# Two mixer layers on one core: the four input projections, three split products or one plain fp32 product

## The chip, the cores and the metric

The kernel runs on one core of a Trainium2 chip. The metric is the device time of one execution in microseconds (us). The core's engines are TensorE (PE in the rows; PEld is its weight load), VectorE (DVE), ScalarE (ACT), GpSimd (POOL) and SyncE (SP, which here only issues DMAs). Each engine runs its own list of instructions in the written order and waits on the others by semaphores.

## The reference, cut to what matters

Two layers over x, 512 tokens of 1024 features, all in fp32. Each layer is a mixer and a feed-forward part:

```python
def hybrid_mixer(x, w_in, ...):
    h = x @ w_in                      # 1024 -> 1824 columns
    (s5_u, g_q, g_k, g_v, g_r, g_lf, g_lb, a_q, a_k, a_v) = jnp.split(h, points, axis=-1)
    y_a = s5_mixer(s5_u, ...)         # state space scan, 256 channels
    y_b = gla_mixer(g_q, g_k, g_v, g_r, g_lf, g_lb, ...)   # gated linear attention, 256
    y_c = swa_mixer(a_q, a_k, a_v, swa_sink)               # windowed attention, 512
    return jnp.concatenate([y_a, y_b, y_c], axis=-1) @ w_out

for l in range(2):
    x = layer_norm(ALPHA * x + hybrid_mixer(x, ...), ...)
    hid = jnp.square(jax.nn.relu(x @ w_ff1[l]))
    x = layer_norm(ALPHA * x + hid @ w_ff2[l], ...)
```

The change touches the product `x @ w_in` alone: how it is computed, and what is kept of x for it.

## The kernel before, in words

**Products.** Nearly all large products are made of three: both operands are split into a high part in a rounded fp32 format (fp32r) and the rest, and `mm3` (lines 251 to 254) adds low x high, high x low and high x high in PSUM. Some small products (the GLU at lines 847 and 851, the gates at line 610, attention times values at line 968) are plain fp32: one `matmul` call on unsplit operands.

**Weights.** `wunit` (lines 237 to 249) brings 1024 columns of weights: a DMA by SyncE into one of two `raw` buffers, a copy by ScalarE into the high half of one of six places in `WA` (line 247, recorded at line 221, the helper `copyA`), and a subtraction by VectorE or GpSimd into the low half (line 248). Which of the two does it is written in the table `CFG`: "g0" to "g3" are the four projections, one letter a unit. The places are used in turn, `state["pair"]` modulo 6.

**The input.** `transpose_x` (lines 256 to 276) transposes a tile of 128 tokens on TensorE, eight blocks of 128, copies each half by ScalarE into `M.XT` (line 265) and subtracts on VectorE (line 266). `M.XT` is two tiles of 16 KB a partition under two of the three rotating tags P, Q, R. The same function serves the feed-forward part, with `sums`.

**The projections.** `proj` (lines 347 to 360) makes one group of columns for all 512 tokens: four weight units, then for each of four token tiles eight blocks of 128 features, each an `mm3`. There are four groups a layer: wg1 (the S5 input and the values of the linear attention, 512 columns), wg0 (its queries, keys and gate inputs, 288), wg2 (keys, values and gate of the two attentions, 512), wg3 (the queries of windowed attention, 512). Their results are taken from PSUM by `evac_g0` to `evac_g2` and `mk_evac_g3`.

**The order.** `CFG["seq"]` (line 39) writes the order of the steps of each mixer: in layer 0 "u st0 g0 tb st1 gates scan scores states sink g2 out g3 y keys late s5o w0 ...". "tb" builds the S5 tables (`tb_params`, `tables`), long chains of small VectorE operations, with a share on GpSimd; those of layer 1 are built during the feed-forward part of layer 0. "st0" and "st1" turn the input into states by the tables, "scan" runs over the states (lines 759 to 764 and on), "gates" and "scores" belong to the linear attention, "keys" and "w0" to "w3" to windowed attention (its first products are at line 933). A planner then orders the instructions of each engine by its own estimate of when each is ready, with the written order as the priority, so the steps overlap.

**Places used by others.** The queries of windowed attention lie in two of the six places, its keys in one, and the weights of `w_out` and of the feed-forward part in all, through the same `wunit`.

Of the kernel before, what the change touches and what calls it, by code (L numbers as in the profile page):

```python
# [20 lines left out]
DEPTH = 2  # L21
# [33 lines left out]
    "sa": "VVVV",  # L55
    "g0": "GGGG",
    "g1": "VVVG",
    "g2": "GVVV",
    "g3": "VVVV",
}  # L60
# [4 lines left out]
def trunk(tc, I, out, dbg=None):  # L65
# [73 lines left out]

    M = NS()  # L140

    def new_lt():
# [94 lines left out]
    def wunit(src, eng=None, cuts=1):  # L237
        n = src.shape[-1]
        raw = rawp.tile([128, 1024], F32, tag="raw", name="raw")
        i = state["pair"] % 6  # L240
        state["pair"] += 1
        for j in range(cuts):
            c = slice(n * j // cuts, n * (j + 1) // cuts)
            nc.sync.dma_start(raw[:, c], src[:, c])
        for j in range(cuts):
            c = slice(n * j // cuts, n * (j + 1) // cuts)
            copyA(WA[:, i, 0, c], raw[:, c])
            (eng or V).tensor_tensor(WA[:, i, 1, c], raw[:, c], WAf[:, i, 0, c], op=SUB)  # L248
        return WA[:, i, 0, :n], WA[:, i, 1, :n]

# [4 lines left out]

    def transpose_x(tt, sums=False):
        for h in range(2):
            ps = psB("xt")
            for k in range(4):
                kk = 4 * h + k  # L260
                T.transpose(ps[:, k * 128:(k + 1) * 128], XR[:, tt, kk * 128:(kk + 1) * 128], ident)
            sl = slice(tt * 128, tt * 128 + 128)
            p4 = ps.rearrange("p (k t) -> p k t", k=4)
            t = M.XT[h]
            state["xt%d" % tt] = S.activation(out=t[:, :, 0, sl], in_=p4, func=AF.Copy)
            V.tensor_tensor(t[:, :, 1, sl], p4, t.bitcast(F32)[:, :, 0, sl], op=SUB)
            if not sums:
                continue
            hs = slice(tt % 2 * 128, tt % 2 * 128 + 128)
# [4 lines left out]
        if sums and tt >= 2:  # L274
            for h in range(2):
                tt_(E("xs", h), Tr[2 + h][:, :, hs], Tr[1][:, :, hs], XF[:, h, :, hs], SUB)
# [69 lines left out]

    def proj(src, n, evac, eng, pre=[]):
        units = pre + [wunit(src[kp], E(eng, kp)) for kp in range(len(pre), 4)]
        for tp in range(2):
            ps = psA("proj")  # L350
            for a in range(2):
                tt = 2 * tp + a
                sl = slice(tt * 128, tt * 128 + 128)
                for k in range(8):
                    w = units[k // 2]
# [534 lines left out]
    def swa_keys(p):  # L890
        kps = psA("kT")
        for tt in range(4):
            for v in range(2):
                T.transpose(kps[:, v, tt * 128:tt * 128 + 128], kdt(tt)[:, v].rearrange("p u d -> p (u d)"), ident)
        KH, KL = [WA[:, p, i].rearrange("p (v t) -> p v t", v=2) for i in range(2)]
        copyA(KH, kps)
        V.tensor_tensor(KL, kps, KH.bitcast(F32), op=SUB)
        return KH, KL
# [137 lines left out]
    def ff1_pair(l, i):  # L1036
# [13 lines left out]
        def unit(src, half=None):  # L1050
            if half != 1:
                u = state["pair"] % 6
# [6 lines left out]
            copyA(WA[:, u, 0, c], src)  # L1059
            V.tensor_tensor(WA[:, u, 1, c], src, WAf[:, u, 0, c], op=SUB)  # L1060
            return WA[:, u, 0, c], WA[:, u, 1, c]

# [92 lines left out]
    pre.append(wunit(I["wg1"][0][1], E("g0", 1), CFG["cut"][1]))  # L1155
    for tt in range(1, 4):
        nc.sync.dma_start(XR[:, tt], I["x"][tt * 128:tt * 128 + 128, :])
    transpose_x(0)
    tb_params()
    run(tb0, 1)  # L1160
    for tt in range(1, 4):
        transpose_x(tt)

# [12 lines left out]
    for l in range(DEPTH):  # L1176
        base = state["pair"] - (2 if l == 0 else 0)
        state["l"] = l
        if l:
            scratch_early()  # L1180
        run(proj(I["wg1"][l], 512, evac_g1, "g0", [] if l else pre))
# [18 lines left out]
        steps = {"u": lambda: s5_u(l), "st0": lambda: s5_states(l, 0), "tb": tb_rest, "st1": lambda: s5_states(l, 1),  # L1200
                 "g0": lambda: run(proj(I["wg0"][l], 288, evac_g0, "g1")), "gates": lambda: gla_gates(l),
                 "scan": lambda: s5_scan(l), "scores": lambda: gla_scores(l), "states": lambda: gla_states(l),
                 "sink": sink, "g2": lambda: run(proj(I["wg2"][l], 512, evac_g2, "g2")), "out": lambda: gla_out(l),
                 "g3": lambda: run(proj(I["wg3"][l], 512, mk_evac_g3(Qs), "g3")), "y": lambda: gla_y(l),
                 "keys": keys, "late": scratch_late, "s5o": lambda: s5_out(l)}
# [15 lines left out]
        def after1(tt):  # L1221
            layer_norm(tt, CFG["ln"][tt])
            transpose_x(tt, True)
        out_half1(ylhs, units, ks, ALPHA, after1)
        new_sums()
        for i in range(3):
            split_sum(i)

        def after2(tt, l=l):
            if l + 1 < DEPTH:  # L1230
                layer_norm(tt, CFG["ln2"][tt])
                transpose_x(tt)
# [110 lines left out]
```

## Time and profile before

| | |
|---|---|
| median of 3 runs | 1246.17 us (1239.97 to 1248.57) |
| profiled execution | 1247.4 us, its span 1245.6 us |
| mean granted TensorE clock | 0.977 of full |
| TensorE busy | 1169.3 us, 94% |
| VectorE busy | 901.5 us, 72% |
| ScalarE busy | 553.4 us, 44% |
| GpSimd busy | 164.1 us, 13% |

Stages in the span: layer 0's mixer runs from 0 to about 240 us, its feed-forward part to about 650, layer 1's mixer to about 870, then the second feed-forward part. A busy TensorE is not TensorE at its peak: matmuls overlap, so the pace of a product is read from the starts of consecutive ones, not from the duration of one.

### The profile page before, as it was taken

The page shows a single profiled execution, that of the slowest core. Times are in us where ns is not written, and L with a number is a line of the kernel's source. Part 1 is how long each engine was busy: PE and PEld are TensorE (multiplying, and loading weights), DVE is VectorE, ACT ScalarE, POOL GpSimd, SP SyncE. Part 2 cuts the span into 40 slices and gives each one's busy share as a digit, 9 for nine tenths or more (in the row PEclk, how much of TensorE's full clock was granted, in tenths as well). Part 3 has the DMA queues.
Part 4 walks back from the last instruction along what each step waited for, and adds up shares of the span by engine and source line. Part 5 has one row for each costly group of instructions (what it writes and reads, how often), then busy time and mean ns, then how long its engine had stood idle before and what let it go on. Part 6 is the DMA issues. An engine that isn't in the chain of part 4 may idle for free.

```text
span 1245.6 us, 18803 instructions
## 1 busy us (share of the span) xinstructions
PE 1169.3 (94%) x7400; PEld 985.5 (79%) x7400; DVE 901.5 (72%) x1727; ACT 553.4 (44%) x937; POOL 164.1 (13%) x123
## 2 busy tenths in 40 slices
PE   6696978999999999999999989799999999999997
PEld 4684765678888889989987867556898898998986
DVE  8986988659875675758564399883987485764957
ACT  4253247534522543725533535572465272461640
POOL 3422352112000000000141020220400000000000
PEclk9898999999999999999999999899999999999999
DMA  6340431113453532412422414302144142250331
GB/s 219 103 153 9 73 123 52 52 34 105 123 166 143 159 104 68 150 54 69 153 82 74 158 34 66 122 17 85 35 138 150 51 142 79 88 164 20 100 121 68
DMA packets 50616, 121.68 MB, mean 98 GB/s; under 512 B 13280, under 2 KB 20320, under 8 KB 50528
## 3 DMA queue, kind: packets, MB, share of 16 engines
q1 hardware_dynamic: 37680, 103.53, 25.2%
q10 hardware_dynamic: 12848, 16.95, 5.3%
q8 instruction: 58, 0.95, 0.3%
q14 instruction: 30, 0.25, 0.1%
HBM read 110.53 MB, written 8.88 MB: 96 GB/s over the span
## 4 chain that ended last, share of the span: by engine, by line
PE 67%; DVE 9%; DMA 2%; ACT 2%; issue 1%; SPq 1%; ACTq 0%; DVEq 0%
PE o L252 11%; PE o L253 11%; PE o L254 11%; PE f1s L252 6%; PE f1s L254 6%; PE f1s L253 6%; PE so L968 2%; PE proj L253 1%; PE proj L254 1%; PE proj L252 1%; PE f1e L253 1%; PE pT L962 1%; PE f1e L254 1%; PE f1e L252 1%; DVE XR L319 1%
## 5 line engine op out<-in xcount | busy, mean ns | idle before, releaser
L221 ACT ACTIVATE WA<-raw 128x1024 fp32r<-128x1024 f32 (+2 forms) x129 | 132.4, 1029 | 140.7 <-DMA raw<-in_w_ff 39.2
L248 DVE TENSOR_TENSOR WA<-raw,WA 128x1024 fp32r<-128x1024 f32 (+1 forms) x102 | 121.8, 1195 | 89.8 <-ACT WA L221 89.8
L221 ACT ACTIVATE WA<-MA 128x1024 fp32r<-128x1024 f32 (+1 forms) x72 | 64.5, 913 | 138.4 <-PE o L254 102.2
L979 DVE SCALAR_TENSOR_TENSOR XR<-XR,o 128x512 f32<-128x512 f32 (+1 forms) x81 | 52.7, 676 | 90.4 <-PE o L254 90.3
L1060 DVE TENSOR_TENSOR WA<-MA,WA 128x1024 fp32r<-128x1024 f32 (+1 forms) x72 | 74.4, 1043 | 17.0 <-ACT WA L221 17.0
L252 PE MATMUL f1s<-xs,WA 128*128 128x256 f32 x288 | 81.6, 283 | 0.2 <-DVE MA L230 0.2
L254 PE MATMUL f1s<-xs,WA 128*128 128x256 f32 x288 | 81.5, 283 | 0.0
L253 PE MATMUL f1s<-xs,WA 128*128 128x256 f32 x288 | 81.5, 283 | 0.0
L248 POOL TENSOR_TENSOR WA<-raw,WA 128x1024 fp32r<-128x1024 f32 (+2 forms) x27 | 61.4, 2280 | 130.0 <-ACT WA L221 123.6
L230 POOL TENSOR_TENSOR XR<-XR,lt 128x512 f32<-128x512 f32 (+1 forms) x13 | 18.5, 1421 | 394.1 <-ACT XR L218 394.1
L230 DVE TENSOR_TENSOR MA<-MA,f1s 128x256 f32<-128x256 f32 x120 | 49.6, 418 | 28.6 <-PE f1s L254 19.6
L252 PE MATMUL o<-WA,yYa 128*128 128x512 f32 (+1 forms) x162 | 64.0, 395 | 0.8 <-DVE XR L979 0.7
L253 PE MATMUL o<-WA,yQ 128*128 128x512 f32 (+1 forms) x164 | 63.4, 386 | 0.0
L252 PE MATMUL o<-WA,yQ 128*128 128x512 f32 (+1 forms) x164 | 63.3, 386 | 0.0
L252 PE MATMUL o<-WA,yYb 128*128 128x512 f32 (+1 forms) x162 | 63.0, 389 | 0.0
L253 PE MATMUL o<-WA,yYa 128*128 128x512 f32 (+1 forms) x162 | 63.0, 389 | 0.0
L253 PE MATMUL o<-WA,yYb 128*128 128x512 f32 (+1 forms) x162 | 63.0, 389 | 0.0
L254 PE MATMUL o<-WA,yYb 128*128 128x512 f32 (+1 forms) x162 | 62.8, 389 | 0.0
L252 PE MATMUL o<-WA,yP 128*128 128x512 f32 x160 | 62.8, 392 | 0.0
L254 PE MATMUL o<-WA,yYa 128*128 128x512 f32 (+1 forms) x162 | 62.7, 387 | 0.0
L254 PE MATMUL o<-WA,yQ 128*128 128x512 f32 (+1 forms) x164 | 62.7, 385 | 0.0
L253 PE MATMUL o<-WA,yP 128*128 128x512 f32 x160 | 62.7, 392 | 0.0
(460 smaller groups left out, 3566.0 us busy)
## 6 DMA issues: line engine op xcount, KB each, us to landing
raw<-in_w_ff SPq DMA_DIRECT2D x80, 512.0 KB, 3.5
MA<-in_w_ff SPq DMA_DIRECT2D x48, 512.0 KB, 3.5
raw<-in_wg SPq DMA_DIRECT2D x23, 512.0 KB, 4.0
raw<-in_w_out SPq DMA_DIRECT2D x16, 512.0 KB, 3.9
scr_out<-MA SPq DMA_DIRECT2D x8, 512.0 KB, 3.7
yc<-scr_out ACTq DMA_DIRECT2D x8, 512.0 KB, 4.4
raw<-in_wg SPq DMA_DIRECT2D x8, 288.0 KB, 2.9
MA<-in_s5cb ACTq DMA_DIRECT2D x8, 256.0 KB, 4.2
```

Of the source, the lines that this page charges most:

```text
L221: S.activation(out=o_, in_=i_, func=AF.Copy)
L230: eng.tensor_tensor(o_, a, b, op=op)
L248: (eng or V).tensor_tensor(WA[:, i, 1, c], raw[:, c], WAf[:, i, 0, c], op=SUB)
L252: T.matmul(ps, a[1], b[0], start=first, stop=False)
L253: T.matmul(ps, a[0], b[1], start=False, stop=False)
L254: T.matmul(ps, a[0], b[0], start=False, stop=last)
L319: V.scalar_tensor_tensor(x[:, c], x[:, c], mean, M.lng[:, c], op0=SUB, op1=MUL)
L962: T.transpose(ps[:, b * 128:b * 128 + 128], P[:, h, b * 128:b * 128 + 128], ident)
L968: T.matmul(ps[64 * v:64 * v + 64, :], av[:, tt - 1 + b0 + b, 64 * v:64 * v + 64], M.pT[v][:, b].rearrange("p h q -> p (h q)"), start=(b == ...
L979: V.scalar_tensor_tensor(x, x, scale, ps, op0=MUL, op1=ADD)
L1060: V.tensor_tensor(WA[:, u, 1, c], src, WAf[:, u, 0, c], op=SUB)
```

## The change

The four projections of both mixers are made of one plain fp32 product for each block, on unsplit operands. The weights of a projection unit go by DMA straight into half a place (`runit`), so a place holds two units, and nothing copies or splits them. The transposed input of a mixer is kept once, in fp32 (`M.XF32`, one 16 KB tile under one tag), by ScalarE's copy alone. The six places become six tiles with tags W0 to W5, so that a place can hold either format; the query places, the key place and the first place of `w_out` are renumbered. The feed-forward part and `w_out` stay in three products.

```diff
-    WA = sb.tile([128, 6, 2, 1024], F32R, name="WA")
-    WAf = WA.bitcast(F32)
...
+    def place(i, dt=F32R):
+
+        return sb.tile([128, 2, 1024], dt, tag="W%d" % (i % 6), name="w%d" % (i % 6))
+
...
+    def runit(src, cuts=1):
+
+        n = src.shape[-1]
+        a = state["half"] % 2
+        if a == 0:
+            state["run"] = place(state["half"] // 2, F32)
+        w = state["run"]
+        state["half"] += 1
+        for j in range(cuts):
+            c = slice(n * j // cuts, n * (j + 1) // cuts)
+            nc.sync.dma_start(w[:, a, c], src[:, c])
+        return w[:, a, :n]
...
+            if not split:
+                state["xt%d" % tt] = S.activation(out=M.XF32[:, 4 * h:4 * h + 4, sl], in_=p4, func=AF.Copy)
+                continue
...
-    def proj(src, n, evac, eng, pre=[]):
-        units = pre + [wunit(src[kp], E(eng, kp)) for kp in range(len(pre), 4)]
+    def proj(src, n, evac, pre=[]):
+        units = pre + [runit(src[kp]) for kp in range(len(pre), 4)]
...
-                    mm3(ps[:, a, :n], xt(k, sl),
-                        (w[0][:, c:c + n], w[1][:, c:c + n]), k == 0, k == 7)
+                    T.matmul(ps[:, a, :n], M.XF32[:, k, tt * 128:tt * 128 + 128], units[k // 2][:, c:c + n],
+                             start=(k == 0), stop=(k == 7))
...
-    new_xt(rot[0:2])
+    M.XF32 = big(rot[0], [128, 8, 512], F32, "xf")
+    state["half"] = 0
...
-    pre.append(wunit(I["wg1"][0][0], E("g0", 0), CFG["cut"][0]))
+    pre.append(runit(I["wg1"][0][0], CFG["cut"][0]))
...
-        base = state["pair"] - (2 if l == 0 else 0)
+        base = state["pair"]
+        if l:
+            state["half"] = 2 * base
...
-        qp = [WA[:, (base + 4 + i) % 6] for i in range(2)]
+        qp = []
 
         def Qs(tt):
+            if tt // 2 == len(qp):
+                qp.append(place(base + 2 + tt // 2))
             return qp[tt // 2][:, tt % 2]
...
-            M.KHL = swa_keys(base % 6)
+            M.KHL = swa_keys((base + 4) % 6)
...
-        state["pair"] = base + 14
+        state["pair"] = base + 5
...
-                transpose_x(tt)
+                transpose_x(tt, False)
...
+                if l + 1 < DEPTH:
+                    M.XF32 = big(rot[1], [128, 8, 512], F32, "xf")
```

The entries "g0" to "g3" of `CFG` go with the splits.

## Rows read from the trace of the kernel before

**Rows 1.** The page's 40 equal slices of the span: busy tenths.

```profile
PE   6696978999999999999999989799999999999997
...
DVE  8986988659875675758564399883987485764957
```

**Rows 2.** Busy us by stage: PE, PEld, DVE, ACT, POOL; clock, DMA share, GB/s.

```profile
0.00:60.00 60.00, 39.57 (x187) 32.41 (x187) 53.58 (x171) 18.74 (x33) 25.84 (x23) 0.95 0.52 167
60.00:114.00 54.00, 48.85 (x502) 42.38 (x502) 40.38 (x69) 25.81 (x51) 14.79 (x11) 0.89 0.27 89
114.00:187.00 73.00, 59.35 (x398) 43.60 (x398) 65.65 (x162) 25.74 (x43) 30.40 (x29) 0.91 0.36 87
...
661.00:715.00 54.00, 53.05 (x391) 45.91 (x391) 15.13 (x26) 24.23 (x44) 4.57 (x3) 0.97 0.39 126
715.00:785.00 70.00, 62.02 (x501) 47.34 (x501) 68.38 (x171) 29.28 (x47) 12.53 (x8) 0.98 0.33 79
```

**Rows 3.** The same for TensorE's instructions on the projections' PSUM tile alone.

```profile
0.00:60.00 60.00, 33.89 (x150) 0.95 0.52 167
60.00:114.00 54.00, 20.68 (x90) 0.89 0.27 89
114.00:187.00 73.00, 37.60 (x144) 0.91 0.36 87
...
661.00:715.00 54.00, 43.72 (x215) 0.97 0.39 126
715.00:785.00 70.00, 37.72 (x145) 0.98 0.33 79
```

**Rows 4.** Prices: from the chain, line 847 alone, the timeline of TensorE, the chain.

```profile
811.21 1.77 PE glg L847 x4
...
L847 PE MATMUL glg<-xl,TAB x16: 592/592/648, 206.9 to 821.3; 128*128 128x512 f32 x16
...
84.81 1.99 PE L610 MATMUL gz<-yb 128*128 128x256 f32 x8
86.46 0.58 PE L253 MATMUL proj<-WA,XTQ 128*128 128x512 f32 x1
...
684.39 0.14 PE proj L252
684.53 0.13 PE proj L253
...
751.25 0.23 PE proj L252
751.48 0.23 PE proj L253
```

**Rows 5.** Subtractions of lines 248 and 266, first 130 us: durations min/median/max, starts, forms.

```profile
L248 DVE TENSOR_TENSOR WA<-raw,WA x8: 750/1216/1225, 31.2 to 84.1; 128x1024 fp32r<-128x1024 f32 x5, 128x576 fp32r<-128x576 f32 x3
...
L248 POOL TENSOR_TENSOR WA<-raw,WA x7: 1263/2361/2433, 5.7 to 51.5; 128x1024 fp32r<-128x1024 f32 x4, 128x512 fp32r<-128x512 f32 x2, 128x576 fp32r<-128x576 f32 x1
...
L266 DVE TENSOR_TENSOR XTP<-xt,XTP x4: 682/684/693, 7.7 to 20.5; 128x512 fp32r<-128x512 f32 x4
```

**Rows 6.** Small VectorE operations in the timeline, two held and one not.

```profile
5.72 1.25 DVE L396 SCALAR_TENSOR_TENSOR yc<-yc 128x32 f32<-128x32 f32 x1
...
51.61 2.37 DVE L485 TENSOR_SCALAR A8S<-APW 128x32 f32<-128x32 f32 x1
...
40.49 0.18 DVE L484 COPY AIS<-APW 128x32 f32<-128x32 f32 x1
```

**Rows 7.** Timelines and line 933: the scan's start, SyncE's loads, ScalarE's wait, the scores.

```profile
114.00 0.61 DVE L761 TENSOR_TENSOR yb<-yc,APW 128x256 f32<-128x256 f32 x1
...
624.10 84.63 SPq L244 DMA_DIRECT2D raw<-in_wg  x16
...
706.05 1.06 ACT L221 ACTIVATE WA<-raw 128x1024 fp32r<-128x1024 f32 x1 [3.25 <-DMA raw<-in_wg]
...
L933 PE MATMUL sc<-WA x32: 362/418/582, 188.1 to 233.7; 128*128 128x256 f32 x16, 128*128 128x384 f32 x16
```

More of the change, by code (lines that the diff above doesn't have):

```diff
@@ L55 @@
     "sa": "VVVV",
[L56 to L59, printed above, removed]
 }
@@ L239, in wunit @@
         raw = rawp.tile([128, 1024], F32, tag="raw", name="raw")
-        i = state["pair"] % 6
+        w = place(state["pair"])
+        wf = w.bitcast(F32)
         state["pair"] += 1
@@ L246, in wunit @@
             c = slice(n * j // cuts, n * (j + 1) // cuts)
-            copyA(WA[:, i, 0, c], raw[:, c])
-            (eng or V).tensor_tensor(WA[:, i, 1, c], raw[:, c], WAf[:, i, 0, c], op=SUB)
-        return WA[:, i, 0, :n], WA[:, i, 1, :n]
+            copyA(w[:, 0, c], raw[:, c])
+            (eng or V).tensor_tensor(w[:, 1, c], raw[:, c], wf[:, 0, c], op=SUB)
+        return w[:, 0, :n], w[:, 1, :n]
+    def runit(src, cuts=1):
[9 more added lines that the diff above has]
+        return w[:, a, :n]
     def mm3(ps, a, b, first, last):
@@ L254, in mm3, with transpose_x @@
         T.matmul(ps, a[0], b[0], start=False, stop=last)
-    def transpose_x(tt, sums=False):
+    def transpose_x(tt, split=True):
+        sl = slice(tt * 128, tt * 128 + 128)
+        hs = slice(tt % 2 * 128, tt % 2 * 128 + 128)
         for h in range(2):
@@ L261, in transpose_x @@
                 T.transpose(ps[:, k * 128:(k + 1) * 128], XR[:, tt, kk * 128:(kk + 1) * 128], ident)
-            sl = slice(tt * 128, tt * 128 + 128)
             p4 = ps.rearrange("p (k t) -> p k t", k=4)
+            if not split:
+                state["xt%d" % tt] = S.activation(out=M.XF32[:, 4 * h:4 * h + 4, sl], in_=p4, func=AF.Copy)
+                continue
             t = M.XT[h]
-            state["xt%d" % tt] = S.activation(out=t[:, :, 0, sl], in_=p4, func=AF.Copy)
+            copyA(t[:, :, 0, sl], p4)
             V.tensor_tensor(t[:, :, 1, sl], p4, t.bitcast(F32)[:, :, 0, sl], op=SUB)
-            if not sums:
-                continue
-            hs = slice(tt % 2 * 128, tt % 2 * 128 + 128)
             if tt < 2:
@@ L273, in transpose_x @@
                 tt_(V, Tr[h][:, :, hs], p4, (XF[:, 0] if h == 0 else Tr[0])[:, :, hs], SUB)
-        if sums and tt >= 2:
+        if split and tt >= 2:
             for h in range(2):
@@ L352, in proj @@
                 tt = 2 * tp + a
-                sl = slice(tt * 128, tt * 128 + 128)
                 for k in range(8):
-                    w = units[k // 2]
                     c = (k % 2) * n
-                    mm3(ps[:, a, :n], xt(k, sl),
-                        (w[0][:, c:c + n], w[1][:, c:c + n]), k == 0, k == 7)
+                    T.matmul(ps[:, a, :n], M.XF32[:, k, tt * 128:tt * 128 + 128], units[k // 2][:, c:c + n],
+                             start=(k == 0), stop=(k == 7))
                 evac(tt, ps[:, a, :n])
@@ L894, in swa_keys @@
                 T.transpose(kps[:, v, tt * 128:tt * 128 + 128], kdt(tt)[:, v].rearrange("p u d -> p (u d)"), ident)
-        KH, KL = [WA[:, p, i].rearrange("p (v t) -> p v t", v=2) for i in range(2)]
+        w = place(p)
+        KH, KL = [w[:, i].rearrange("p (v t) -> p v t", v=2) for i in range(2)]
         copyA(KH, kps)
@@ L1051, in unit @@
             if half != 1:
-                u = state["pair"] % 6
+                u = place(state["pair"])
                 state["pair"] += 1
@@ L1058, in unit @@
             c = slice(0, 1024) if half is None else slice(512 * half, 512 * half + 512)
-            copyA(WA[:, u, 0, c], src)
-            V.tensor_tensor(WA[:, u, 1, c], src, WAf[:, u, 0, c], op=SUB)
-            return WA[:, u, 0, c], WA[:, u, 1, c]
+            copyA(u[:, 0, c], src)
+            V.tensor_tensor(u[:, 1, c], src, u.bitcast(F32)[:, 0, c], op=SUB)
+            return u[:, 0, c], u[:, 1, c]
         wa, w12, w3 = unit(r1), unit(s12), unit(r2)
@@ L1152, in trunk @@
     nc.sync.dma_start(XR[:, 0, 0:512], I["x"][0:128, 0:512])
-    pre.append(wunit(I["wg1"][0][0], E("g0", 0), CFG["cut"][0]))
+    pre.append(runit(I["wg1"][0][0], CFG["cut"][0]))
     nc.sync.dma_start(XR[:, 0, 512:], I["x"][0:128, 512:])
-    pre.append(wunit(I["wg1"][0][1], E("g0", 1), CFG["cut"][1]))
+    pre.append(runit(I["wg1"][0][1], CFG["cut"][1]))
     for tt in range(1, 4):
         nc.sync.dma_start(XR[:, tt], I["x"][tt * 128:tt * 128 + 128, :])
-    transpose_x(0)
+    transpose_x(0, False)
     tb_params()
@@ L1180, in trunk @@
             scratch_early()
-        run(proj(I["wg1"][l], 512, evac_g1, "g0", [] if l else pre))
+        run(proj(I["wg1"][l], 512, evac_g1, [] if l else pre))
         if l == 0:
             run(tb0, 2)
-        qp = [WA[:, (base + 4 + i) % 6] for i in range(2)]
+        qp = []
         def Qs(tt):
+            if tt // 2 == len(qp):
+                qp.append(place(base + 2 + tt // 2))
             return qp[tt // 2][:, tt % 2]
@@ L1200, in trunk @@
         steps = {"u": lambda: s5_u(l), "st0": lambda: s5_states(l, 0), "tb": tb_rest, "st1": lambda: s5_states(l, 1),
-                 "g0": lambda: run(proj(I["wg0"][l], 288, evac_g0, "g1")), "gates": lambda: gla_gates(l),
+                 "g0": lambda: run(proj(I["wg0"][l], 288, evac_g0)), "gates": lambda: gla_gates(l),
                  "scan": lambda: s5_scan(l), "scores": lambda: gla_scores(l), "states": lambda: gla_states(l),
-                 "sink": sink, "g2": lambda: run(proj(I["wg2"][l], 512, evac_g2, "g2")), "out": lambda: gla_out(l),
-                 "g3": lambda: run(proj(I["wg3"][l], 512, mk_evac_g3(Qs), "g3")), "y": lambda: gla_y(l),
+                 "sink": sink, "g2": lambda: run(proj(I["wg2"][l], 512, evac_g2)), "out": lambda: gla_out(l),
+                 "g3": lambda: run(proj(I["wg3"][l], 512, mk_evac_g3(Qs))), "y": lambda: gla_y(l),
                  "keys": keys, "late": scratch_late, "s5o": lambda: s5_out(l)}
@@ L1222, in after1 @@
             layer_norm(tt, CFG["ln"][tt])
-            transpose_x(tt, True)
+            transpose_x(tt)
         out_half1(ylhs, units, ks, ALPHA, after1)
@@ L1231, in after2 @@
                 layer_norm(tt, CFG["ln2"][tt])
-                transpose_x(tt)
+                transpose_x(tt, False)
             else:
```

## The prediction

> **What bounds the kernel now.** I read the page's 40 slices first. They show that outside the two mixers TensorE is at nine tenths or more, while in the mixers (the first seven slices and slices 21 to 27) TensorE falls to six and seven tenths and VectorE rises to nine [rows 1]. The table by stage says which engine holds which part [rows 2]. In layer 0 VectorE is busy 53.6 of the first 60 us: it builds the S5 tables there, a chain of small operations. The scan of the S5 states, which needs those tables, begins at 114.0 us [rows 7]. From 114 to 187 both engines are near full: VectorE 65.7 and TensorE 59.4 of 73 us. At 188.1 the first attention scores start [rows 7]. In layer 1 there are no tables to build in the mixer: TensorE alone is full from 661 to 715 (53.1 of 54 us, VectorE 15.1), and from 715 to 785 VectorE leads (68.4 of 70) with TensorE at 62.0 [rows 2]. So the change trades time on one near-full engine for time on the other, and the answer differs by stage.
>
> The same table for the projections alone [rows 3] counts what stands where. A layer has 4 projections x 4 token tiles x 8 blocks = 128 products of three instructions, 384. In layer 0, 240 of these (80 products: all of the first two projections and 16 of the third) come before 114 us, 144 (48 products) after it. In layer 1, 145 (48) come after 715 and 239 (80) before.
>
> **The price of a product.** Three split instructions of 512 columns start 0.23 us apart [rows 4]: 0.69 us a product. With 288 columns they are 0.133 apart on average [rows 4]: 0.40. A plain fp32 product stands in the trace in the GLU: four rows of line 847 take 1.77 us, 0.4425 each [rows 4]. But the source has 2 layers x 2 halves x 2 blocks = 8 such products and the trace has 16 rows [rows 4]: one plain product is two instructions. So it costs 0.885 us, not 0.4425. For 288 columns no row exists. Eight rows of 256 columns (four products) take 1.65 us up to the next projection product, 0.206 each [rows 4]; by columns that is 0.23 for 288, and from the 512 row 0.25. I take 0.24, so 0.48 a product, bounds 0.46 and 0.50. TensorE therefore gains no time, it loses it: per layer 96 x (0.885 - 0.69) + 32 x (0.48 - 0.40) = 18.7 + 2.6 = 21.3 us, and 42.6 us in all.
>
> The Trainium skill (Perfetto Trace Analysis, section Engine Utilization) gives the array's output rate with a factor of one half for its two-part fp32 mode. Read per product, that would be near 0.44 us and the whole change would free TensorE; read per instruction it agrees with the 0.4425 us row, and the count of 16 rows decides for the second reading. The first is kept as the fourth case below.
>
> **What is removed.** Per layer: 16 copies on ScalarE (about 1.05 us, 0.69 for the narrow ones; off the path nearly everywhere), the subtractions behind them, and 8 subtractions of the transposed input on VectorE (0.68 us each; four of the eight are shown) [rows 5]. In layer 0 before the scan VectorE loses 8 weight subtractions, five of 1.22 and three of 0.75 us [rows 5], and those 8: with the small overlap that back-to-back rows show, about 12.5 us. GpSimd loses seven [rows 5], and these cost VectorE too: while one runs, a VectorE operation of 0.18 us takes 1.25 or 2.37 us [rows 6]: the first two rows there are the first and the last of those that were held, the third a free one. Over the seven subtractions I count such excess as 1.1, 1.0, 2.1, 2.2, 1.9, 1.1 and 2.2, about 11 us; the least it could be worth is nothing, if another GpSimd operation takes the place. VectorE's part of the table chain is so 12.5 to 24 us shorter, and I take 24: every held operation is a link of that chain.
>
> **Layer 0.** By VectorE alone the scan starts at 114 - 24 = 90 us. TensorE must keep up: of its 88.4 us before 114 [rows 2] 54.6 are projections [rows 3], so 33.8 are other work. New: 32 x 0.885 + 32 x 0.48 + 33.8 = 77.5 us, against some 84 that lie between the first loads (about 6 us, an estimate) and 90. That fits, with room for 7 products of the third projection instead of 16. The second stage then has 48 + 9 = 57 products, 50.4 us, beside 59.4 - 37.6 = 21.8 us of other work: 72.2 us of TensorE. VectorE needs about 63 there (65.7 less two subtractions). How long the stage lasts hangs on how well TensorE is packed. At the share of before (59.4 of 73, 81%) it is 89 us; at the 98% that TensorE reaches from 661 to 715 it is 74. I take 90%, 80 us. The scores would begin at about 170 instead of 187: **-17 us**, bounds -8 and -23.
>
> **Layer 1.** The start gains a little: the first products no longer wait for a subtraction after each copy, nor for the weights' split, and the GpSimd subtractions leave the layer norm ahead of them. On the other side the first two projections take 32 x 0.195 + 32 x 0.08 = 8.8 us more of a full TensorE. Up to 715 the projections had 49.7 us there, 6.0 before 661 (the remaining 24 instructions, by the same pace) and 43.7 after [rows 3]; the 64 products now need 43.7, so about 7 to 9 of the third projection fit instead of 16. The gates get 3 us back: ScalarE's copy of a weight at 706.05 sat 3.25 us waiting for its load, with the gates queued behind it on that engine [rows 7]. I put the start of the scan 3 us earlier. After it come 55 products, 48.7 us, plus 62.0 - 37.7 = 24.3: 73.0 us of TensorE. At before's 88.6% that is 82.4 us, at 98% 74.5, at 93% 78.5 against 70 now. Together **+5.5 us**, bounds +1.5 and +9.4.
>
> **What moves and what waits.** The 16 weight loads of a layer go straight into the six places, two to a place, where before each went through a ring of two buffers, and SyncE sat 84.6 us over the 16 loads of layer 1 [rows 7]. A load now waits for the last product that read its place. By the count of places (layer 1 begins at place 92, so 2, 3, 4, 5, 0, 1, 2, 3 modulo six) the first projection's weights are in before the layer norm ends; the second's wait for the end of the last feed-forward product, some 20 us ahead of use. Behind a waiting load on SyncE stand only later weights, table stores and parameter loads, none due within that time. I put it at 0, with up to 4 us lost if a store is held. The query places and the key place are freed no later than before.
>
> **Sum.** -17 + 5.5 = -11.5 us against the profiled execution of 1247.4 us (its span 1245.6): 1235.9. That execution lies 1.2 us above the median of 1246.17, inside the spread of the runs. I forecast 1236.
>
> **Rivals.** *VectorE decides throughout (faster).* The other work on TensorE fits into its holes at once: the second stage of layer 0 keeps its 73 us, so -24, and layer 1 gets -3 from the gates and -2.3 from two subtractions after 715: -29, 1218 us. For it: VectorE's 98% from 715 to 785. Against it: TensorE's sum of 72 to 73 us for each of those stages, which asks for a packing that it had only where VectorE was idle.
>
> *TensorE's order decides (slower).* The planner writes one order for TensorE. If it puts the table transposes behind the longer products, the scan starts at 104, not 90, and if the holes stay where they are the stage lasts 89 us: 193, +6. In layer 1 the same costs 12.4 us plus some 3 at the start: +15. Together +21, 1268 us. It decides once layer 0's scan starts after about 97 us. For it: TensorE is already at 93% from 661 to 785. Against it: in the table stage VectorE is the one that is late.
>
> *The table chain is not shorter.* GpSimd's own table work stretches into the freed time and only the 12.5 us of VectorE's subtractions are won: 11.5 us less gain, 1247 us, no change.
>
> *Half price.* If a product were 0.4425 us, TensorE would lose 13 us of its own stage in layer 1 and VectorE would decide the rest: -29 - 13, about 1205 us.
>
> **Chances.** Forecast 0.50 (its own range 1226 to 1247: the two pairs of bounds give 1226 and 1249), VectorE throughout 0.20, TensorE's order 0.17, chain not shorter 0.10, half price 0.03. About 1% (12.5 us) is what a measurement here can tell from no change. Of the forecast I put two fifths beyond 1%: faster 0.20 + 0.03 + 0.19 = 0.42, slower 0.17, same 0.41. The range 1214 to 1259 leaves out the half price, most of the slow case and little else.
>
> **What would show it.** Right: the plain products appear as two rows each, 0.44 us apart, 512 rows in all; the scan of layer 0 (line 761 before) starts near 90 us; TensorE is over 88% in the second stage of both layers; layer 1's scan to scores is longer than before. Wrong: a scan start after 97, a second stage of layer 0 under 74 or over 89 us, or a layer 1 that is shorter by more than 5 us.

## The result, and the profile after

The changed kernel takes 1290.14 us (median of 4 runs, 1286.58 to 1292.98) where the kernel before, run beside it, takes 1246.6: a ratio of 1.0358, 95% interval 1.0307 to 1.0408. It is slower by 44 us, outside the range given and on the other side of the forecast of 1236. The profiled execution has a span of 1284.5 us, 38.9 more than before.

The page's slices of the changed kernel, to be read against [rows 1]:

```profile
PE   7987798999999999999999994899999999999997
...
DVE  7926949649885766648550197785787586574957
```

In the early slices the nines of before have gone from VectorE (8986988 is now 7926949), as intended. TensorE is fuller there, but has a hole of four tenths in slice 25, right after VectorE's own hole of 0 and 1 in slices 23 and 24. The two engines now take turns in layer 1: first TensorE full and VectorE empty, then the other way round.

The same in the table by stage of the changed kernel, cut at its own scans and scores (columns as in [rows 2]):

```profile
0.00:60.00 60.00, 50.09 (x187) 28.97 (x188) 51.37 (x186) 13.48 (x28) 18.24 (x21) 0.94 0.71 250
60.00:109.90 49.90, 44.00 (x423) 31.42 (x421) 18.20 (x39) 19.09 (x41) 9.38 (x6) 1.00 0.06 18
109.90:193.30 83.40, 68.77 (x348) 34.18 (x348) 62.82 (x145) 24.39 (x40) 29.06 (x29) 0.88 0.26 57
664.00:742.90 78.90, 78.90 (x370) 45.02 (x369) 12.34 (x35) 22.40 (x47) 2.56 (x4) 1.00 0.23 80
742.90:814.60 71.70, 54.86 (x310) 27.79 (x310) 58.92 (x136) 20.28 (x33) 9.11 (x6) 0.88 0.29 59
```

From 60 us to the scan VectorE's busy time fell from 40.4 [rows 2] to 18.2 us, and still the scan of layer 0 starts only 4 us earlier than before (109.9 against 114.0). In layer 1 TensorE is without a gap from 664.0 to 742.9, with VectorE busy 12.3 of 78.9 us.

Three of the four stages (mixer of layer 0, its feed-forward part, mixer of layer 1; each mixer is cut at the first products of the feed-forward part, so that it holds `w_out` too), first before, then after:

```profile
0.00:290.30 290.30, 246.25 (x1609) 187.08 (x1609) 234.66 (x558) 125.73 (x262) 93.23 (x77) 0.94 0.31 92
290.30:650.60 360.30, 358.07 (x2175) 316.64 (x2174) 251.42 (x400) 155.64 (x219) 18.93 (x10) 1.00 0.35 115
650.60:891.50 240.90, 221.77 (x1445) 169.03 (x1443) 172.03 (x386) 114.95 (x239) 46.80 (x33) 0.96 0.27 78
```

```profile
0.00:300.60 300.60, 262.43 (x1480) 163.86 (x1481) 209.75 (x540) 112.09 (x245) 78.69 (x70) 0.95 0.28 88
300.60:664.00 363.40, 360.44 (x2190) 318.80 (x2188) 252.56 (x406) 153.94 (x219) 14.01 (x10) 1.00 0.37 120
664.00:931.10 267.10, 241.28 (x1302) 148.16 (x1301) 158.61 (x363) 103.59 (x223) 36.67 (x27) 0.95 0.21 61
```

Layer 0's mixer is 10.3 us longer, layer 1's 26.2, the first feed-forward part 3.1 (the last, not shown, is 0.7 shorter). This is the most useful reading of the case: subtract TensorE's busy time from each mixer. Idle were 290.3 - 246.25 = 44.1 and 240.9 - 221.77 = 19.1, together 63.2 us; idle are now 38.2 and 25.8, together 64.0. VectorE lost 25 + 13 us of work in the mixers, and TensorE's idle time did not shrink. Over both mixers, all that TensorE gained in work (16.2 + 19.5 us) went into the span one for one: layer 0 gave 5.9 us of its idle time back, layer 1 added 6.7.

Where the planner let TensorE run ahead, in the timelines of the changed kernel. In layer 0 twenty rows stand before the small table products (`lag`), and VectorE waits 8.9 us for those. In layer 1 eighteen rows stand before the last products that turn the input into states (`sv`), and the scan (line 772) waits for ScalarE's copy of their result:

```profile
67.20 7.63 PE L368 MATMUL proj<-w,xf 128*128 128x512 f32 x20
74.76 0.41 PE L587 MATMUL lag<-MA 128*32 128x128 f32 x2
...
733.26 7.89 PE L368 MATMUL proj<-w,xf 128*128 128x512 f32 x18
741.08 1.15 PE L754 MATMUL sv<-lt,TAB 128*64 128x64 f32 x32
```

```profile
76.87 0.69 DVE L569 TENSOR_TENSOR MA<-yc 128x512 f32<-128x512 f32 x1 [8.92 <-PE lag L589]
...
742.28 0.60 ACT L219 ACTIVATE yc<-sv 128x512 f32<-128x512 f32 x1 [1.59 <-PE sv L754]
...
742.91 0.63 DVE L772 TENSOR_TENSOR yb<-yc,APW 128x256 f32<-128x256 f32 x1 [0.76 <-ACT yc L219]
```

### The profile page after: what moved, and what is told of

It is laid out like the page before. It is cut to its first block, busy times and chain, and to the rows that moved or that the text cites. A ratio compares the mean times of both kernels' runs of the same rounds, so it can differ in the third digit from the quotient of the medians.

```text
span 1284.5 us, 18126 instructions
## 1 busy us (share of the span) xinstructions
PE 1207.2 (94%) x7144; PEld 943.5 (73%) x7144; DVE 864.3 (67%) x1691; ACT 526.4 (41%) x904; POOL 134.5 (10%) x110
## 4 chain that ended last, share of the span: by engine, by line
PE 75%; DVE 17%; DMA 3%; ACT 2%; issue 1%; SPq 1%; ACTq 0%; DVEq 0%
PE o L264 11%; PE o L265 11%; PE o L266 11%; PE proj L368 9%; PE f1s L264 6%; PE f1s L266 6%; PE f1s L265 6%; PE so L980 2%; PE f1e L265 1%; PE f1e L266 1%; PE f1e L264 1%; DVE SM__80 L952 1%; PE pT L974 1%; DVE yc L804 1%; DVE yc L775 1%
## 5 line engine op out<-in xcount | busy, mean ns | idle before, releaser
L368 PE MATMUL proj<-w,xf 128*128 128x512 f32 (+1 forms) x512 | 208.1, 559 | 0.7 <-ACT xf L278 0.7
L368 PEld LDWEIGHTS proj<-w,xf 128*128 128x128 f32 x512 | 97.1, 194 | 93.3 <-issue 83.8
L247 DVE TENSOR_TENSOR w<-raw,w 128x1024 fp32r<-128x1024 f32 x82 | 100.2, 1223 | 59.6 <-ACT w L219 59.4
L219 ACT ACTIVATE w<-raw 128x1024 fp32r<-128x1024 f32 x96 | 101.4, 1059 | 91.6 <-PE o L266 38.3
L1072 DVE TENSOR_TENSOR w<-MA,w 128x1024 fp32r<-128x1024 f32 (+1 forms) x72 | 74.5, 1043 | 16.6 <-ACT w L219 16.6
L264 PE MATMUL f1s<-xs,w 128*128 128x256 f32 x288 | 81.6, 283 | 0.3 <-DVE MA L228 0.3
L266 PE MATMUL f1s<-xs,w 128*128 128x256 f32 x288 | 81.5, 283 | 0.0
L265 PE MATMUL f1s<-xs,w 128*128 128x256 f32 x288 | 81.5, 283 | 0.0
L264 PE MATMUL o<-w,yYa 128*128 128x512 f32 (+1 forms) x162 | 63.8, 394 | 2.0 <-ACT MA L216 1.3
L265 PE MATMUL o<-w,yQ 128*128 128x512 f32 (+1 forms) x164 | 63.4, 386 | 0.0
L264 PE MATMUL o<-w,yQ 128*128 128x512 f32 (+1 forms) x164 | 63.3, 386 | 0.0
L265 PE MATMUL o<-w,yYa 128*128 128x512 f32 (+1 forms) x162 | 63.1, 390 | 0.0
L264 PE MATMUL o<-w,yYb 128*128 128x512 f32 (+1 forms) x162 | 63.1, 390 | 0.0
L265 PE MATMUL o<-w,yYb 128*128 128x512 f32 (+1 forms) x162 | 63.1, 389 | 0.0
L264 PE MATMUL o<-w,yP 128*128 128x512 f32 x160 | 63.0, 394 | 0.0
L266 PE MATMUL o<-w,yYb 128*128 128x512 f32 (+1 forms) x162 | 62.8, 388 | 0.0
L266 PE MATMUL o<-w,yQ 128*128 128x512 f32 (+1 forms) x164 | 62.7, 385 | 0.0
L266 PE MATMUL o<-w,yYa 128*128 128x512 f32 (+1 forms) x162 | 62.7, 387 | 0.0
L265 PE MATMUL o<-w,yP 128*128 128x512 f32 x160 | 62.6, 391 | 0.0
```

The source lines that it names most:

```text
L219: S.activation(out=o_, in_=i_, func=AF.Copy)
L247: (eng or V).tensor_tensor(w[:, 1, c], raw[:, c], wf[:, 0, c], op=SUB)
L264: T.matmul(ps, a[1], b[0], start=first, stop=False)
L265: T.matmul(ps, a[0], b[1], start=False, stop=False)
L266: T.matmul(ps, a[0], b[0], start=False, stop=last)
L368: T.matmul(ps[:, a, :n], M.XF32[:, k, tt * 128:tt * 128 + 128], units[k // 2][:, c:c + n], start=(k == 0), stop=(k == 7))
```

## The experiments

The theory after this reading, called *price*: the end follows TensorE's work, and the plain products cost what their rows say. Its rival, called *order*: the products have come to stand ahead of the small products that the scan waits for, and another order would give the loss back. Several kernels below make a product of bf16 instructions, which read the upper 16 bits of each fp32 word. Where there are several to a product, each adds the same product again, so that only TensorE's time is changed by their number.

**Price with the splits gone.** The changed kernel, each plain product replaced by three cheap bf16 instructions on the same unsplit tiles:

```diff
-                    T.matmul(ps[:, a, :n], M.XF32[:, k, tt * 128:tt * 128 + 128], units[k // 2][:, c:c + n],
-                             start=(k == 0), stop=(k == 7))
+                    for r in range(3):
+                        T.matmul(ps[:, a, :n], M.XF32.bitcast(BF16)[:, k, tt * 256 + 1:tt * 256 + 256:2],
+                                 units[k // 2].bitcast(BF16)[:, 2 * c + 1:2 * c + 2 * n:2],
+                                 start=(k == 0 and r == 0), stop=(k == 7 and r == 2))
```

> The changed kernel with each plain product replaced by three bf16 instructions on the same unsplit tiles (the high half of every fp32 word; low bits are left out). Weights still go by DMA into their places and nothing is split, so this is the relief without the dearer product. Theory 'price' (a product of 0.885 us instead of 0.69 lies on TensorE's path): about 1240 us, 1228 to 1248, that is all of the 44 us come back and the relief shows. Theory 'order' (weights that are ready early let the planner put products of the third projection ahead of the gates): it keeps at least half of the loss, 1265 or more.

1242.2 us, ratio 0.997 (0.9951 to 0.999). The change without its price gains 4 us. The scan of layer 0 starts at 95.0:

```profile
L774 DVE TENSOR_TENSOR yb<-yc,APW x7: 604/617/623, 95.0 to 114.3; 128x256 f32<-128x256 f32 x7
```

**Price with the splits kept.** The kernel before, one plain product on the high halves (the products with a low half are left out), all copies and subtractions still made:

```diff
-                    mm3(ps[:, a, :n], xt(k, sl),
-                        (w[0][:, c:c + n], w[1][:, c:c + n]), k == 0, k == 7)
+                    T.matmul(ps[:, a, :n], xt(k, sl)[0].bitcast(F32), w[0][:, c:c + n].bitcast(F32),
+                             start=(k == 0), stop=(k == 7))
```

> The kernel before with one plain fp32 product on the high halves in place of the three (the low halves are still made, but not used). The dearer product without the relief. Theory 'price': 1246 + 42 us of TensorE, less what falls into its idle time, 1275 to 1290. Theory 'order': a product still waits for its weights' copy, so the planner's order stays near that of before and the loss is under 25 us, 1255 to 1270.

1295.66 us, ratio 1.0405 (1.0371 to 1.044). The four kernels make a square: the price is 49 us with the splits (1295.7 - 1246.3) and 48 without (1290.1 - 1242.2); the relief is 4 us at the old price and 5.5 at the new. The two terms add, and the relief is a tenth of the price. (One corner differs in format too: its three instructions are bf16, those of `mm3` fp32r. Their paces are close, 0.227 us in the run with four below and 0.23 in [rows 4].)

**Another order.** The changed kernel, its third projection held on TensorE until the gates' products are through:

```diff
+        def held(name, ev):
+            with tc.issue_after(state["gs"].ins):
+                run(proj(I[name][l], 512, ev))
...
-                 "sink": sink, "g2": lambda: run(proj(I["wg2"][l], 512, evac_g2)), "out": lambda: gla_out(l),
+                 "sink": sink, "g2": lambda: held("wg2", evac_g2), "out": lambda: gla_out(l),
```

> The changed kernel with the products of the third projection queued on TensorE behind the last cumulative-sum product of the gates (line 631), in both layers. Theory 'order': the gates and the scan of layer 1 start some 20 us earlier and the whole gets back 12 to 25 us, 1265 to 1278. Theory 'price': TensorE has the same sum of work, so it moves by less than 8 us, 1282 to 1298.

1290.36 us, ratio 1.0359 (1.0328 to 1.0391): nothing. Layer 1's scan did start 13.8 us earlier (729.1 against 742.9), but its scores came later (826.1 against 814.6): the products held back now lie between the two, 128 rows in place of 74. Rows of this run, the scan's and the scores' of layer 1, then the projections' tile alone, up to layer 0's scan and between layer 1's scan and scores:

```profile
L772 DVE TENSOR_TENSOR yb<-yc,APW x7: 607/616/1355, 729.1 to 749.7; 128x256 f32<-128x256 f32 x7
...
L945 PE MATMUL sc<-w,w x32: 362/402/687, 826.1 to 875.8; 128*128 128x256 f32 x16, 128*128 128x384 f32 x16
...
0.00:111.80 111.80, 62.34 (x160) 31.38 (x160) 0.00 (x0) 5.06 (x14) 0.94 0.40 143
...
729.10:826.10 97.00, 59.04 (x128) 24.69 (x128) 2.72 (x8) 5.43 (x12) 0.92 0.25 55
```

In layer 0 the edit moved nothing out of the way: 160 rows still stand ahead of the scan, as in the changed kernel (whose rows stand in the section on why the prediction was wrong), and it starts at 111.8. So this other order of layer 1, at least, gives nothing back; another order of layer 0 was not tried.

**Load without fp32.** One, two and four bf16 instructions a product, by the count in the loop of the first experiment. In the run with four, 28 of them follow each other on TensorE's timeline, the last 0.39 us long: (6.51 - 0.39) / 27 = 0.227 each. So four cost 0.907, against 0.859 for a plain product of the changed kernel (16 rows from 664.00 until the next transpose at 670.87):

```profile
665.86 6.51 PE L369 MATMUL proj<-w,xf 128*128 128x512 bf16 x28
```

```profile
664.00 7.03 PE L368 MATMUL proj<-w,xf 128*128 128x512 f32 x16
670.87 1.04 PE L275 MATMUL xt<-CS,XR 128*128 128x128 f32 x8
```

> The changed kernel with four bf16 instructions of full width for each product of the four projections (on the high halves of the unsplit words, so the low bits are left out of the computation), where the run with three took 1242. Four at the pace of three (0.23 us each at 512 columns, 0.133 at 288) cost 0.92 and 0.53 us a product, about what the plain fp32 product costs (0.885, 0.48); nothing else of the fp32 form is left. Price theory (the end follows TensorE's added time and nothing else of fp32): 26 us more a layer than three instructions, so 1242 + 53 = 1295, range 1288 to 1303. Rival, the fp32 form itself costs more than its rows (loads of wide weights, a clock that falls): four cheap instructions then stay well under the changed kernel's 1290, at 1255 to 1280.

> The changed kernel with one bf16 instruction for each product of the four projections (a third of the run with three, low bits left out of the computation): 2 x (96 x 0.46 + 32 x 0.27) = 105 us of TensorE less. Price theory, TensorE still the bound in both mixers at three instructions: the span falls by most of it, 1242 - 105 = 1137 at the least and about 1155 when layer 0 ends on VectorE's 212 us. Rival, at before's price VectorE already decides in the mixers: 1220 to 1240.

> The changed kernel with two bf16 instructions per product of the projections (low bits left out of the computation), between the runs with one (1206), three (1242) and four (1276): by the paces 52.6 us of TensorE more than one. Theory: the mixers have idle time on TensorE only up to some load and from there on every us counts, so the curve bends: 1216 to 1222. Rival, a straight line through one and three, as if each instruction had the same share hidden: 1224, 1223 to 1227. If VectorE still decided at two: 1205 to 1212.

One 1206.35 us (ratio 0.969, 0.9661 to 0.9718), two 1222.56 (0.9825, 0.9796 to 0.9855), three 1242.2, four 1275.59 (1.0239, 1.0219 to 1.0259). Each instruction more is some 52 us of TensorE by its pace, and the time grows by 16, 20 and 33 us. So neither expectation for one instruction was right: at a low load two thirds of the added work disappear in idle time, at the load of the change one third. Whether the curve already bends between one and three, the run with two can't say: its runs (1219.9 to 1226.1) cover both expectations. And four instructions a product are 15 us faster than the plain one, though they cost TensorE no less. Price alone doesn't explain the changed kernel.

The scan of layer 0 in the run with one, then with two, where TensorE has more room (it comes back in the account of the prediction):

```profile
L774 DVE TENSOR_TENSOR yb<-yc,APW x7: 602/611/624, 88.3 to 110.9; 128x256 f32<-128x256 f32 x7
...
L774 DVE TENSOR_TENSOR yb<-yc,APW x7: 605/617/622, 86.0 to 106.7; 128x256 f32<-128x256 f32 x7
```

**Grain.** The changed kernel, each plain product cut into two of half the columns:

```diff
+                    for r in range(2):
+                        h = slice(r * n // 2, (r + 1) * n // 2)
+                        T.matmul(ps[:, a, h], M.XF32[:, k, tt * 128:tt * 128 + 128],
+                                 units[k // 2][:, c:c + n][:, h], start=(k == 0 and r == 0), stop=(k == 7 and r == 1))
```

> The changed kernel with every plain fp32 product of the projections cut into two of half the columns (256 or 144), the whole computation kept. By the rows of before a 256-column product is two instructions of 0.206 to 0.221 us, so two halves cost 0.825 to 0.885 where the whole one costs 0.885: TensorE's sum is the same or up to 2 x 96 x 0.06 = 11.5 us less. The changed kernel is 15 us slower than four bf16 instructions a product, with the same busy time of TensorE and 13 us more idle time. If the coarse grain makes that (a small matmul waits behind instructions of 0.44 us that the planner cannot put it between), finer products bring it back: 1270 to 1281. If it is one order's accident, or belongs to fp32 products as such: 1284 to 1296.

1271.47 us, ratio 1.0214 (1.0186 to 1.0243): 18.7 us of the loss come back with the computation unchanged. The products are still fp32, so these 18.7 us do not belong to fp32 as such; nor are two halves cheaper at 512 columns (16 rows from 654.73 until the transpose at 658.18, 0.216 us each, 0.862 for both):

```profile
654.73 3.62 PE L370 MATMUL proj<-w,xf 128*128 128x256 f32 x16
658.18 1.04 PE L275 MATMUL xt<-CS,XR 128*128 128x128 f32 x8
```

The mixers of this run:

```profile
0.00:288.60 288.60, 259.14 (x1737) 204.04 (x1737) 206.06 (x540) 111.95 (x245) 78.10 (x70) 0.96 0.30 92
...
653.00:911.90 258.90, 240.66 (x1558) 189.97 (x1557) 156.29 (x363) 102.35 (x223) 36.96 (x27) 0.97 0.22 64
```

TensorE is busy 499.8 us in the two (503.7 in the changed kernel) and idle 29.5 + 18.2 = 47.7 (64.0). With four bf16 instructions it is idle 50.2:

```profile
0.00:290.80 290.80, 260.38 (x1723) 162.82 (x1737) 206.62 (x540) 112.69 (x245) 78.81 (x70) 0.97 0.30 91
...
654.60:920.30 265.70, 245.92 (x1545) 150.72 (x1557) 159.28 (x363) 103.76 (x223) 37.76 (x27) 0.96 0.21 62
```

Two kernels with fine products stand at 1271 and 1276, three with coarse ones at 1290 to 1296, whatever their splits and order. That makes the grain a likely cause of some 15 us, but it is not shown apart from the order: finer products also give the planner another one. Ahead of layer 1's scan 294 rows stand here, 73.5 products, where the changed kernel has 91:

```profile
653.00:717.30 64.30, 53.74 (x294) 47.05 (x294) 0.71 (x2) 5.05 (x14) 1.00 0.29 98
```

Which waits the grain lengthens was not isolated either.

**Layer by layer.** Plain products in one layer, three bf16 instructions in the other:

```diff
+                    if state["l"] == 0:
+                        T.matmul(ps[:, a, :n], M.XF32[:, k, tt * 128:tt * 128 + 128], units[k // 2][:, c:c + n],
+                                 start=(k == 0), stop=(k == 7))
+                        continue
+                    for r in range(3):
...
```

> The changed kernel with plain fp32 products in layer 0 only; layer 1's projections are three bf16 instructions per product on the unsplit words (the low bits of layer 1's projections are left out). If each layer pays its own price: layer 0 as in the changed kernel (its second layer begins at 664), then layer 1 as in the run with three (245.5 + 353.3): span 1263, 1264 to 1270 us in all. If layer 0's loss is taken back in layer 1, or most of it is layer 1's: 1245 to 1255. If layer 0 has nearly all of it: above 1280.

> The counterpart of the run with plain fp32 in layer 0 alone (1271.6): plain fp32 products in layer 1 only, three bf16 instructions per product in layer 0 (the low bits of layer 0's projections are left out). If the layers' prices add: 1290.1 - 1271.6 = 18.5 us over the run with three (1242.2), so 1261, range 1257 to 1265. If what is over the 42.6 us of the sum is an accident of one order, the two do not add: outside 1253 to 1270.

In layer 0 alone 1271.6 us (ratio 1.0216, 1.0193 to 1.024), in layer 1 alone 1264.89 (1.0152, 1.0129 to 1.0174). Against the run with three, layer 0's plain products cost 29.4 us and layer 1's 22.7, together 52 where both at once cost 48. Both layers pay, layer 0 alone a little above its expected range; the sum holds within 4 us.

**What GpSimd's subtractions hold.** The run with three instructions, plus seven subtractions on GpSimd as before the change:

```diff
+        if state["half"] in (1, 2, 3, 4, 8, 9):
+            raw = rawp.tile([128, 1024], F32, tag="raw", name="raw")
+            for j in range(cuts):
+                c = slice(n * j // cuts, n * (j + 1) // cuts)
+                G.tensor_tensor(raw[:, c], w[:, a, c], w[:, a, c], op=SUB)
```

> The run with three bf16 instructions (unsplit inputs, low bits left out of the computation) plus seven subtractions on GpSimd in layer 0, of the size and at the places of those that the change removed (first projection's four weights, one of the second, one of the third), into the ring of buffers that nothing reads. My step said that they hold VectorE's table chain by 11 us: the scan of layer 0 then starts at about 106 instead of 95.0, and the end of layer 0's mixer is about 8 to 11 us later than 273.7. Rival, the holding is hidden (another operation was late anyway): scan start 95 to 97, and the time stays at 1242.

1251.67 us (ratio 1.0052, 1.0035 to 1.0069), 9.5 more than without. The scan starts at 102.0, 7 us later, where 11 were expected; these subtractions together take GpSimd 11.1 us, those of before 13.5, and they lie earlier. The timelines of this run show the holding itself: the VectorE operations of 0.18 us take 1.02 while GpSimd's two-operand subtraction runs.

```profile
5.22 1.02 DVE L412 TENSOR_SCALAR yc<-PSR 128x32 f32<-128x32 f32 x1 [4.00 <-DMA PSR<-in_s5p]
6.27 0.18 DVE L401 TENSOR_SCALAR yc<-yc 128x32 f32<-128x32 f32 x1
...
7.04 1.02 DVE L402 TENSOR_SCALAR yc<-yc 128x32 f32<-128x32 f32 x1
```

```profile
5.16 1.04 POOL L265 TENSOR_TENSOR raw<-w 128x512 f32<-128x512 f32 x1 [3.33 <-DMA w<-in_wg]
6.93 1.09 POOL L265 TENSOR_TENSOR raw<-w 128x512 f32<-128x512 f32 x1 [0.74 <-DMA w<-in_wg]
```

The kernel before with those subtractions given to VectorE:

```diff
-    "g0": "GGGG",
-    "g1": "VVVG",
-    "g2": "GVVV",
+    "g0": "VVVV",
+    "g1": "VVVV",
+    "g2": "VVVV",
```

> The kernel before with GpSimd's seven weight subtractions of each layer given to VectorE (g0, g1 and g2 all V); nothing else changed. If what they cost is that they hold VectorE (7 us at the scan of layer 0 when they were added alone), then VectorE pays 7 x 1.2 = 8.5 us for them itself and wins 7 to 11: scan start 112 to 116 where before has 114.0, the time within 3 us of 1246. If the holding were worth more than the subtractions themselves, the scan would start at 104 to 108 and the time be 1238 to 1241.

The scan starts at 114.0, as in before, to the tenth; the time is 1268.49 us (ratio 1.0192, 1.0168 to 1.0215), 24 us worse. The same instructions on TensorE (7400 rows in each) are busy 1183.1 us here and 1169.3 before, at a mean granted clock of 0.964 and 0.977, and its idle time is 7 us more. The loss is behind layer 0's scan (its mixer ends at 298.9 instead of 290.3) and in layer 1 (251.8 us instead of 240.9), though the work is the same; that it comes from the order that follows is the likely reading, not shown apart from the clock. So an edit of a few microseconds can move this kernel by twenty, and neither the relief of 4 us is to be read as the worth of the subtractions, nor the 19 us of the halves as the worth of the grain alone.

**A faster version.** The runs point to fewer instructions, not to fewer splits. Beside the run with one bf16 instruction (1206.35), the kernel before with only the product of the two rounded high halves:

```diff
-            (eng or V).tensor_tensor(WA[:, i, 1, c], raw[:, c], WAf[:, i, 0, c], op=SUB)
+            if low:
+                (eng or V).tensor_tensor(WA[:, i, 1, c], raw[:, c], WAf[:, i, 0, c], op=SUB)
...
-                    mm3(ps[:, a, :n], xt(k, sl),
-                        (w[0][:, c:c + n], w[1][:, c:c + n]), k == 0, k == 7)
+                    T.matmul(ps[:, a, :n], xt(k, sl)[0], w[0][:, c:c + n], start=(k == 0), stop=(k == 7))
```

> The kernel before with only the third of each product's three instructions (high half by high half, rounded by ScalarE's copies), and no subtraction for the projections' weights or the mixers' transposed input: the two products with a low half are left out of the computation. TensorE has 105 us less by the paces (0.46 us a wide product, 0.27 a narrow one), VectorE what the change removed. The run with one bf16 instruction took 1206, with scans at 90.7 and 672.7. Theory (VectorE's chains set the mixers once TensorE is relieved; ScalarE's copies are hidden): 1203 to 1212, at the scans the same. Rival (the direct loads and the missing copies had a share in that gain): 1215 to 1230, with the first scan after 96.

1218.63 us, ratio 0.9788 (0.9763 to 0.9813), scans at 96.7 and 692.4. It beats both kernels, with less precise projections; the version with bf16 and direct loads is 12 us faster still. So the direct loads and missing copies are probably worth something where TensorE has room, as the rival said; the two also differ in format. (The first scan of that version starts at 88.3, not at the 90.7 of the expectation, whose view began at 90; the rival fits as before.) No version that keeps the whole product was found to beat the kernel before: even the change at about the old price (three cheap instructions) gains only 4 us.

## Why the prediction was wrong, step by step

*The price held.* 512 rows, two a product, 0.43 us apart where 0.4425 was taken, and 0.253 at 288 columns (ten rows from 715.74 to 718.27) where 0.24 was; the case of half price is out. The reading per instruction of the Trainium skill's factor (Perfetto Trace Analysis, section Engine Utilization) is the one that the count bears out. TensorE's busy time grew by 37.9 us (1207.2 - 1169.3) where the sum had 42.6. The loads, put at 0, held too: in the trace of the changed kernel TensorE waits for the projections' weights 1.0 us in all.

*The relief of the tables held in its place.* By VectorE alone the scan of layer 0 was to start at 90. With one cheap instruction a product it starts at 88.3, with two at 86.0: the 24 us were there, where TensorE has room. With three it starts at 95.0, so the 5 us that are missing there come with TensorE's load. The part of GpSimd in the 24 was counted as 11 and moved the scan by 7 when it was put back, with shorter subtractions and at that load.

*The step that failed first is that the plain products fit ahead of the scan.* "That fits, with room for 7 products of the third projection instead of 16" took it that TensorE would do what the scan needs and no more, without a gap. The planner put as many ahead as before, each now longer. The changed kernel's rows for the projections' tile alone:

```profile
0.00:109.90 109.90, 62.92 (x160) 30.69 (x160) 0.00 (x0) 5.03 (x14) 0.97 0.41 145
109.90:193.30 83.40, 44.45 (x96) 18.78 (x96) 2.68 (x8) 4.59 (x10) 0.88 0.26 57
664.00:742.90 78.90, 67.95 (x182) 33.83 (x182) 2.14 (x6) 6.58 (x18) 1.00 0.23 80
742.90:814.60 71.70, 32.21 (x74) 13.73 (x74) 0.68 (x2) 2.56 (x5) 0.88 0.29 59
```

160 rows are 80 products before the scan of layer 0, the 80 of [rows 3]; in layer 1 it is 182, or 91, where 80 stood before it. Hence 109.9 in place of 90, and in layer 1 a scan 78.9 us after the mixer's start where before took 64.8 (650.6 to 715.4). The gain of 3 us from the gates could not show. All of TensorE up to the scan of layer 0, in the changed kernel and in the run with three cheap instructions, which has some 80 products there too:

```profile
0.00:109.90 109.90, 94.09 (x608) 60.39 (x608) 69.56 (x224) 32.57 (x69) 27.62 (x27) 0.97 0.41 145
```

```profile
0.00:95.00 95.00, 80.54 (x683) 52.87 (x688) 69.59 (x222) 32.68 (x69) 27.48 (x27) 0.96 0.48 167
```

The 15 us between the two scans are the price: 94.1 us of work against 80.5, with about the same idle time. Of the 20 us between forecast and result, some 10 are work (94.1 where 77.5 and 7 products, 83.7, were counted) and some 10 idle time (15.8 where the forecast left the 6 of the first loads).

*The second step, on which the time hangs, is the packing.* The forecast put TensorE at 90% in the second stage of layer 0 and at 93% in that of layer 1. They are 82% (68.77 of 83.4) and 77% (54.86 of 71.7). A sum over both layers would have shown how much was asked: TensorE's idle time of 63.2 us in the mixers, plus 42.6 us of new work, in 11.5 us less time, leaves 63.2 - 42.6 - 11.5 = 9 us idle. It was 64.0. The run with the other order shows that this weighs more than the first step. In its layer 1 the scan starts 61.4 us after the mixer's start (667.7 to 729.1), as the forecast had it (64.8 - 3 = 61.8), and yet the mixer lasts 263.2 us where before took 240.9. TensorE is idle 20.5 of them, where the forecast's +5.5 would leave 19.1 + 5.5 - 21.3 = 3.3:

```profile
667.70:930.90 263.20, 242.65 (x1303) 150.74 (x1301) 158.89 (x363) 102.83 (x223) 38.75 (x27) 0.96 0.22 63
```

*The third is that a scan started earlier is an end reached earlier.* In the run with three instructions layer 0's scan is 19 us early, its mixer ends 16.6 early (273.7 against 290.3), layer 1 begins 10.9 early, and the end is 7.1 early in the profile, 4 by the medians. So the relief, which the rival "VectorE decides throughout" put at 29 us, is worth 4, and the price, which the forecast let cost 29 - 11.5 = 17.5, costs 48.

*Of the rivals,* TensorE's order was the nearest in sign and in its point: the scan starts after 97, the second stage lasts 83.4 us and the scores come at 193.3, where it said 193. That the 193 agrees is luck: it added 104 and 89, and they were 109.9 and 83.4. It had +6 in layer 0 (10.3 measured for the whole mixer) and +15 in layer 1 (26.2). It too left out the grain, and it named a cause that another order of layer 1 did not mend: the price is most of it. By the medians the 44 us are +29 for the price in fine products (1271.5 - 1242.2), +19 for their grain and the order that comes with it (1290.1 - 1271.5, not shown apart) and -4 for the relief.

## What to carry to other kernels

Before counting on a busy engine to absorb new work, write down the idle time that the forecast leaves it, over the whole stretch, and ask for a reason why it should fall from what the trace shows; here 63 us would have had to become 9. Work taken from the engine that is late at one place is worth what arrives at the end: follow it to the end of the span, not to the next milestone. And count a product's instructions by rows of the trace: the call written once was two instructions, and dearer than the three that it replaced.

## What the runs showed of the hardware that was not expected

After the longer idle times here TensorE's granted clock is low, and its holes so cost more than their length. Stretches of layer 1 of the changed kernel (columns as in [rows 2]):

```profile
762.00:772.00 10.00, 9.51 (x23) 3.92 (x22) 9.31 (x37) 3.11 (x5) 0.00 (x0) 1.00 0.00 0
775.20:777.40 2.20, 2.07 (x4) 0.59 (x4) 2.19 (x5) 0.00 (x0) 0.00 (x0) 1.00 0.00 0
782.00:792.00 10.00, 2.07 (x8) 1.78 (x8) 9.03 (x24) 3.17 (x6) 1.26 (x1) 0.50 0.27 75
792.50:796.30 3.80, 3.77 (x8) 1.26 (x12) 0.73 (x1) 0.00 (x0) 0.00 (x0) 0.50 1.17 158
```

```profile
775.28 2.07 PE L656 MATMUL gsc<-MA 128*128 128x512 f32 x4 [1.42 <-DVE MA L657]
784.54 2.07 PE L641 MATMUL gb<-CS,ya 128*128 128x128 f32 x8 [7.18 <-DVE MA L657]
792.53 3.75 PE L656 MATMUL gsc<-MA 128*128 128x512 f32 x4 [5.92 <-issue]
```

Four rows of `gsc` take 2.07 us after an idle time of 1.4 us, at a granted clock of 1.00, and another four of the same form 3.75 us after two idle times of 7.2 and 5.9, at 0.50 (the lower level, 1.2 GHz). Busy time thus holds some of the price of idleness. The 13.8 us more of busy time for the same TensorE instructions in the run with the subtractions on VectorE, at a lower mean clock, fit this; that the clock makes all of them was not shown.
